# A diffusion backbone on one core: scan products in a written order, like tile shapes together, no fill-in products

## Chip, core and metric

The kernel runs on one core of one Trainium2 chip. The metric is the device time of one execution in microseconds (us), shown as the median of three runs. Engines are named as in the profile: PE is TensorE's matmuls and PEld its weight loads, DVE is VectorE, ACT is ScalarE, POOL is GpSimd, SP is SyncE, which issues the DMAs.

## What is computed

Four layers over 256 latent and 256 context tokens of width 1024; layer i has the mixer i mod 3 (attention, RWKV-7 time mixing, pooling), each followed by a squared-ReLU MLP. The change lies in layer 1, RWKV-7, whose core is a recurrence over the tokens, run forwards and backwards for 16 heads of 64 channels:

```
def step(state, inp):
    r_t, w_t, k_t, v_t, kk_t, a_t = inp
    sa = jnp.einsum("bhvk,bhk->bhv", state, kk_t)
    state = (state * w_t[:, :, None, :]
             - sa[..., None] * (kk_t * a_t)[:, :, None, :]
             + v_t[..., None] * k_t[:, :, None, :])
    return state, jnp.einsum("bhvk,bhk->bhv", state, r_t)

for d in range(N_DIRS):
    rev = d == 1
    s_ctx, yc = _wkv_scan(zero, r_c, dec_c[d], key_c[d], v_c, kk_c, a_c[d], rev)
    _, yl = _wkv_scan(s_ctx, r_l, dec_l[d], key_l[d], v_l, kk_l, a_l[d], rev)
```

The two directions' outputs are summed, normalised per head (a group norm), given a bonus term and a gate, and multiplied by an output matrix.

## The kernel before, in words

`rwkv_scan` does the recurrence in chunks of 64 tokens. Work is cut into 16 units n: for each of 8 pairs of heads (`cc`), first the context half (s = 1), then the latent half (s = 0). A unit has both heads, both directions and 4 chunks (`q`); within a chunk the recurrence becomes products of 64x64 matrices and one triangular inverse. A unit passes through stages, and the loop over n works on five units at a time: in iteration n stand, in this order, `levels` of unit n+1, `chain` of n, `front_c` of n+2, `finish_a` of n, `chunks` of n+1, `front_b` of n+3, `front_a` of n+4 and the group norm of n (`STAGES`).

- `front_a` (L907) makes decays and keys: small products, Tanh and Exp on ACT, a running sum `cum` on DVE.
- `front_b` (L947) makes `KB` and `AR`, their products (`pre<-AR,KB`, L961) and the masked matrices `NG` (L966), which go to DRAM. `base` (L1008) reads their 16x16 diagonal blocks back, inverts them by small DVE operations (L1025 to L1034) and fetches the result as `X` and `XT`.
- `front_c` (L971) transposes `KB`, `AR` and the values (L982 to L996).
- `levels` (L1044) first makes a product of `VU` and `NG` (L1061), copied into `XR`; then it widens the inverse in two levels (L1057): `inv<-X,NG`, masked into `Tm`, then `inv<-XT,Tm` (and `inv<-Tm,XT`), by which DVE updates `XT` (L1082, once per level) and `X`.
- `chunks` (L1086) multiplies `XR` by `XT` (L1094) in two halves; ACT copies each to `G` and, scaled, to `VU` (L1097, L1099); `inv<-NG,G` (L1103) gives `P` and `Rp` on DVE (L1109, L1110); then `Q` (L1117, L1119) and the first part of the output sum `yps` (L1124).
- `chain` (L1129) carries the state `S` over the 4 chunks: a product on PE (L1142), an update on DVE (L1147), a product into `yps` (L1151).
- `finish_a` (L1155) centres the output and takes its variance; `inverse_std` and `finish_b` (L1168, L1173) finish the group norm after every second pair of heads (at n = 3, 7 and 11), and after each of the last two pairs; an ACT table load stands ahead of them.

A tile scheduler orders each engine's queue; the program's order of stages is only its preference, so products of different stages alternate in PE's queue. `warm` (L876) puts in 128x256 products whose result nobody reads (L880, the fill-in products): 2 after L1061, 3 after `inv<-X,NG`, 4 after `inv<-XT,Tm` and 3 after each product of the chain (`WARM`). The `inv` products share two PSUM banks, the `pre` products two, `lora` has one. After the scan `rwkv_output` multiplies the gated output by the output matrix (`pre<-kvr,KB` and `pre<-kvr,AR`, L248); the scheduler lets its first products run among the scan's last iterations.

Below, **P** is the start of DVE's first L1109 of a unit and **XT2** the end of DVE's second L1082.

Of the kernel before, what the change touches and what calls it, by code (L numbers as in the profile page):

```python
# [6 lines left out]
F32 = mybir.dt.float32  # L7
# [13 lines left out]
class Kern:  # L21
# [793 lines left out]
    def rwkv_scan(self, R, W, U, ps, psu, K, V, Rr, hid, xr):  # L815
# [19 lines left out]
        g = lambda dd: 1 - dd  # L835
# [46 lines left out]
        with self.pool("rwDram", 1, space=bass.MemoryType.DRAM) as dr:  # L882
# [24 lines left out]
            def front_a(cc, s, w2):  # L907
# [6 lines left out]
                nc.vector.scalar_tensor_tensor(kkn, kc[:, sl], v["k_k"][:, cc:cc + 1], pk[:, :T], op0=ALU.mult, op1=ALU.mult)  # L914
                tw = W.tile([128, 2, T], F32, name="tw")
# [29 lines left out]
                return dict(kkn=kkn, E=E, lam=lam, iL=iL, key=key, b=ta)  # L945

            def front_b(cc, s, st, it):  # L947
# [4 lines left out]
                NG = U.tile([128, 2, 2, 4, 3, 64], F32, name="NG", tag="NG", bufs=2)  # L952
                for dd in range(2):
# [4 lines left out]
                    nc.gpsimd.tensor_mul(AR[:, :, 1, g(dd)], tv(Rr[cc][:, s * T:s * T + T]), E[:, dd, :, 1:65])  # L958
                for dd in range(2):
# [8 lines left out]
                    nc.sync.dma_start(full(Ls[it % NB], g(dd)), NG[rows(g(dd)), dd, :, :, 0].rearrange("p h q x -> p (h q) x"))  # L968
                st.update(AR=AR, KB=KB, NG=NG)

            def front_c(cc, s, st):  # L971
# [7 lines left out]
                for dd in range(2):  # L979
# [4 lines left out]
                    nc.scalar.copy(NG[:, dd, :, :, 2], pn.rearrange("p q (h x) -> p h q x", h=2))  # L984
                pn = pt().rearrange("p (q x) -> p q x", q=4)
# [3 lines left out]
                nc.scalar.copy(XR[:, :, :, 0], pn.rearrange("p q (h x) -> p h q x", h=2))  # L989
                vr = W.tile([128, T], F32, name="vr", tag="t1")  # L990
# [6 lines left out]
                for dd in range(2):  # L997
                    for par in range(2):
                        nc.scalar.copy(VU[rows(dd), dd, par::2].rearrange("p q h x -> p q (h x)"), pv[rows(par), dd])
                ks = W.tile([128, T], F32, name="ks")  # L1000
# [5 lines left out]
                st.update(XR=XR, VU=VU)  # L1006
# [36 lines left out]

            def levels(st):  # L1044

                NG, VU, XT, X, XR = [st[n] for n in ("NG", "VU", "XT", "X", "XR")]
# [3 lines left out]
                def bank():  # L1050
                    return psu.tile([128, 2, 4, 64], F32, name="inv", tag="inv", bufs=2)
# [7 lines left out]
                p = bank()  # L1059
                for dd, hh, q in units:  # L1060
                    nc.tensor.matmul(p[rows(g(dd)), hh, q], lhsT=NG[rows(dd), dd, hh, q, 0], rhs=VU[rows(dd), dd, q, hh],  # L1061
                                     start=True, stop=True)
                warm("k")
                nc.scalar.copy(XR[:, :, :, 1], p)
                for lv, m in enumerate((16, 32)):
# [10 lines left out]
                    else:  # L1076
                        nc.scalar.mul(cols(Tz, 0), cols(p, 0), odd[:, 0:1])
                    p = prod(of(Tz), of(XT))
# [4 lines left out]
                    if lv == 0:  # L1083
                        nc.vector.tensor_sub(cols(X, 0), cols(X, 0), cols(p2, 0))

            def chunks(st):  # L1086
# [3 lines left out]
                for hh in range(2):  # L1090
# [7 lines left out]
                    for dd in range(2):  # L1098
                        nc.scalar.mul(VU[rows(g(dd)), dd, :, hh], p[rows(g(dd)), :, 1], -1.0)  # L1099
                P = U.tile([128, 2, 4, 64], F32, name="P", tag="P", bufs=2)  # L1100
# [10 lines left out]
                p = psu.tile([128, 2, 4, 64], F32, name="inv", tag="inv", bufs=2)  # L1111
                Q = U.tile([128, 2, 4, 64], F32, name="Q", tag="Q", bufs=2)
                yp = psu.tile([128, 2, T], F32, name="yps", tag="yps", bufs=1)
                for dd in range(2):
                    for q in range(4):
                        for hh in range(2):
                            nc.tensor.matmul(p[rows(hh), dd, q], lhsT=NG[:, dd, hh, q, 2], rhs=VU[:, dd, q, hh],  # L1117
                                             start=True, stop=True)
                nc.vector.tensor_mul(Q, p, st["lam"].unsqueeze(3).broadcast_to([128, 2, 4, 64]))  # L1119
                start = [True, True]  # L1120
                for dd in range(2):
                    for q in range(4):
                        for hh in range(2):
                            nc.tensor.matmul(yp[rows(hh), dd, q * 64:q * 64 + 64], lhsT=VU[:, dd, q, hh],  # L1124
                                             rhs=NG[:, dd, hh, q, 1], start=start[hh], stop=True, skip_group_check=True)
                            start[hh] = False
                st.update(P=P, Rp=Rp, Q=Q, yp=yp)

            def chain(st, s, S):  # L1129
                P, Rp, Q, yp, lam = [st[n] for n in ("P", "Rp", "Q", "yp", "lam")]  # L1130
                for q in range(4):
                    if s == 1 and q == 0:
                        S = U.tile([128, 2, 64], F32, name="S", tag="S", bufs=3)
                        nc.gpsimd.tensor_copy(S, Q[:, :, 0])
                        continue
                    So = S
                    if not (s == 0 and q == 3):
# [8 lines left out]
                        for dd in range(2):  # L1146
                            nc.vector.scalar_tensor_tensor(S[:, dd], p[:, dd], lam[:, dd, q:q + 1], Q[:, dd, q],  # L1147
                                                           op0=ALU.mult, op1=ALU.add)
                    for dd in range(2):
# [3 lines left out]
                return S  # L1153

            def finish_a(cc, s, yp, y2):  # L1155
# [4 lines left out]
                nc.vector.tensor_add(y, y, yp[:, 1, ::-1])  # L1160
                yp = pt(0).rearrange("p (a t) -> p a t", a=2)
                nc.tensor.matmul(yp[:, 0], lhsT=c["center"], rhs=y, start=True, stop=True)
                nc.scalar.square(y, yp[:, 0])
                nc.scalar.copy(y2[0][:, sl], yp[:, 0])
                nc.tensor.matmul(yp[:, 1], lhsT=c["meanH"], rhs=y, start=True, stop=True)
                return nc.scalar.copy(y2[1][:, sl], yp[:, 1])
# [6 lines left out]
            def finish_b(cc, w2, y2, r):  # L1173
# [7 lines left out]
                nc.gpsimd.tensor_add(y, y, V[cc])  # L1181
                pf = pt(0)
# [242 lines left out]
```

## Time and profile before

| | |
|---|---|
| median of 3 runs | 2548.38 us (2546.79 to 2548.97) |
| the profiled execution | 2542.58 us |
| its span in the profile | 2540.7 us |
| PE busy / DVE / ACT / POOL, share of the span | 95% / 68% / 43% / 13% |
| fill-in products: first start, last start | 849.0 us, 1358.2 us |

The span is the time in which the engines work; the execution is 1.9 us longer. The table's busy shares are averages over layers with different limits: PE's 95% comes mostly from the long dense products of the MLPs. The scan takes about a fifth of the span.

### The profile page before, as it was taken

What the parts mean: (1) busy time and instruction counts of PE and PEld (TensorE: products, weight loads), DVE (VectorE), ACT (ScalarE), POOL (GpSimd) and SP (SyncE); (2) the same over time, 40 slices, a digit from 0 to 9 for tenths busy, and PEclk for the clock granted to TensorE, in tenths of its full rate; (3) what the DMA queues carried; (4) which work ended last, traced back from release to release, by engine and by line L of the source; (5) the groups of instructions that cost most, each with busy time, mean ns of one, the idle gap of its engine ahead of it and who ended that gap; (6) DMA issues with size and microseconds to landing.
All of it is one profiled execution on the core that took longest, in us unless ns stands there. A gap on an engine that the chain in (4) does not pass through costs nothing.

```text
span 2540.7 us, 42517 instructions
## 1 busy us (share of the span) xinstructions
PE 2418.3 (95%) x17392; PEld 1941.5 (76%) x17392; DVE 1723.3 (68%) x2813; ACT 1101.3 (43%) x2015; POOL 341.5 (13%) x406
## 2 busy tenths in 40 slices
PE   7999999999799999999999899999899999898999
PEld 5556888888577777777777788888788888766999
DVE  5777787674786666666664777664787683787555
ACT  4677523323564334343443523323533323476443
POOL 0110101100202222222210101100011001010110
PEclk9999999999899999999999999999899999999999
DMA  7530355553123311211132255452155553203453
GB/s 276 187 112 32 131 198 187 188 185 116 60 83 96 73 37 38 38 32 37 32 69 99 84 199 198 166 183 85 68 196 182 184 197 116 72 26 108 166 181 135
DMA packets 154834, 308.36 MB, mean 121 GB/s; under 512 B 107152, under 2 KB 111632, under 8 KB 122768
## 3 DMA queue, kind: packets, MB, share of 16 engines
q1 hardware_dynamic: 154640, 305.65, 35.7%
q8 instruction: 137, 2.24, 0.4%
q14 instruction: 57, 0.47, 0.1%
HBM read 294.58 MB, written 11.03 MB: 120 GB/s over the span
## 4 chain that ended last, share of the span: by engine, by line
PE 80%; DVE 11%; ACT 6%; issue 2%; POOL 1%; DMA 1%; SPq 0%; DVEq 0%; ACTq 0%; POOLq 0%
PE mm L248 51%; PE mm L259 3%; PE warm L880 2%; PE inv L1057 2%; PE po L618 2%; PE pre L248 2%; PE pre L961 2%; DVE wL L238 1%; PE pt L613 1%; PE sc L602 1%; PE rps L870 1%; PE inv L1103 1%; ACT wH L237 1%; PE yps L1124 1%; DVE cum L930 1%
## 5 line engine op out<-in xcount | busy, mean ns | idle before, releaser
L238 DVE TENSOR_TENSOR wL<-wraw,wH 128x1024 fp32r<-128x1024 f32 (+1 forms) x364 | 415.1, 1144 | 270.6 <-ACT wH L237 269.7
L237 ACT CAST wH<-wraw 128x1024 fp32r<-128x1024 f32 (+1 forms) x364 | 341.8, 943 | 448.0 <-PE mm L248 425.8
L248 PE MATMUL mm<-hH,wH 128*128 128x512 f32 (+1 forms) x1296 | 471.0, 364 | 2.3 <-ACT wH L237 2.1
L248 PE MATMUL mm<-hH,wL 128*128 128x512 f32 (+1 forms) x1296 | 470.7, 363 | 2.5 <-DVE wL L238 2.4
L248 PE MATMUL mm<-hL,wH 128*128 128x512 f32 (+1 forms) x1296 | 465.6, 360 | 0.0
L248 PE MATMUL mm<-uH,wH 128*128 128x512 f32 (+1 forms) x1072 | 380.6, 355 | 0.0
L248 PE MATMUL mm<-uL,wH 128*128 128x512 f32 (+1 forms) x1072 | 379.4, 355 | 0.3
L248 PE MATMUL mm<-uH,wL 128*128 128x512 f32 (+1 forms) x1072 | 379.5, 354 | 0.0
L188 DVE SCALAR_TENSOR_TENSOR acc<-wraw,sc_sb,acc 128x2048 f32<-128x2048 f32 x126 | 302.2, 2414 | 51.6 <-DMA wraw<-in_w_mod 46.3
L379 POOL TENSOR_TENSOR usq<-relu 128x512 f32<-128x512 f32 (+1 forms) x128 | 144.5, 1130 | 1252.6 <-ACT relu L377 1252.6
L248 PEld LDWEIGHTS mm<-hH,wH 128*128 128x128 f32 x1296 | 244.8, 189 | 56.0 <-ACT wH L237 11.7
L248 PEld LDWEIGHTS mm<-hH,wL 128*128 128x128 f32 x1296 | 244.9, 189 | 42.8 <-DVE wL L238 5.1
L248 PEld LDWEIGHTS mm<-hL,wH 128*128 128x128 f32 x1296 | 244.7, 189 | 35.8 <-issue 0.2
L248 PEld LDWEIGHTS mm<-uL,wH 128*128 128x128 f32 x1072 | 202.3, 189 | 29.1 <-DVE uL L383 1.1
L248 PEld LDWEIGHTS mm<-uH,wH 128*128 128x128 f32 x1072 | 202.7, 189 | 28.4
L248 PEld LDWEIGHTS mm<-uH,wL 128*128 128x128 f32 x1072 | 202.7, 189 | 28.3
L326 DVE SCALAR_TENSOR_TENSOR x<-mm,mod,x 128x256 f32<-128x256 f32 x272 | 121.9, 479 | 132.3 <-PE mm L248 132.1
L377 ACT ACTIVATE relu<-mm 128x512 f32<-128x512 f32 (+1 forms) x128 | 69.2, 544 | 296.4 <-PE mm L248 283.3
L259 PE MATMUL mm<-hH,wH 128*128 128x256 f32 (+1 forms) x232 | 75.5, 328 | 26.4 <-ACT hH L309 15.4
L382 ACT CAST uH<-usq 128x512 fp32r<-128x512 f32 (+1 forms) x128 | 72.7, 569 | 46.1 <-POOL usq L379 46.1
L383 DVE TENSOR_TENSOR uL<-usq,uH 128x512 fp32r<-128x512 f32 (+1 forms) x128 | 80.4, 629 | 0.8
L880 PE MATMUL warm<-busy 128*128 128x256 f32 x400 | 77.3, 318 | 0.0
(342 smaller groups left out, 3906.9 us busy)
## 6 DMA issues: line engine op xcount, KB each, us to landing
wraw<-in_w_mod SPq DMA_DIRECT2D x96, 1024.0 KB, 4.9
wraw<-in_w_in SPq DMA_DIRECT2D x64, 1024.0 KB, 5.8
wraw<-in_w_out SPq DMA_DIRECT2D x64, 1024.0 KB, 5.8
wraw<-in_w_qk SPq DMA_DIRECT2D x10, 1024.0 KB, 4.8
wraw<-in_w_rkv SPq DMA_DIRECT2D x9, 1024.0 KB, 4.8
wraw<-in_w_ao SPq DMA_DIRECT2D x16, 512.0 KB, 4.0
Ls<-NG SPq DMA_DIRECT2D x32, 128.0 KB, 2.6
XT<-Xs SPq DMA_DIRECT2D x32, 128.0 KB, 3.2
```

The source lines that it names most:

```text
L188: nc.vector.scalar_tensor_tensor(acc, raw, self.sc[:, k, s:s + 1], acc, op0=ALU.mult, op1=ALU.add)
L237: nc.scalar.copy(h[:, sl], raw[:, sl])
L238: nc.vector.tensor_sub(l[:, sl], raw[:, sl], h[:, sl].bitcast(F32))
L248: self.nc.tensor.matmul(ps, lhsT=a[:, k], rhs=b, start=(n == 0), stop=(n == 3 * nk - 1))
L259: self.nc.tensor.matmul(ps[:, lo:hi], lhsT=a[:, k], rhs=b, start=(k == z == 0), stop=(k == nk - 1 and z == 2))
L326: self.nc.vector.scalar_tensor_tensor(self.x[o][:, a:b], ps, G[:, o, s:s + 1], self.x[o][:, a:b], op0=ALU.mult, op1=ALU.add)
L377: nc.scalar.activation(r[:, :n], ps[:, :n], AF.Relu)
L379: nc.gpsimd.tensor_mul(u2[:, :n], r[:, :n], r[:, :n])
L382: nc.scalar.copy(uH[:, :n], u2[:, :n])
L383: nc.vector.tensor_sub(uL[:, :n], u2[:, :n], uH[:, :n].bitcast(F32))
L618: nc.tensor.matmul(po[hf * 64:hf * 64 + 64], lhsT=vn[:, k0 + kc, (2 * P + hf) * 64:(2 * P + hf) * 64 + 64], rhs=pts[hf][:, kc].rearrange(" ...
L880: self.tc.keep_in_program_order(nc.tensor.matmul(wb[:, 0:T], lhsT=busy[:, 0:128], rhs=busy, start=True, stop=True))
```

## The change

The stages become generators that stop after each step (`yield`), and a list `STEPS` names, step by step, the order in which an iteration takes them; `k` is now the first product of `levels`, cut out as a step of its own (`mv`), and `G` the gate product of the group norm, taken in the next iteration. From iteration 0 on, `ordered` ties each PE instruction to the one before, so PE's queue follows the list; the other engines' queues are still ordered by the scheduler. `WARM` is empty: none of the 400 fill-in products is left. Everything computed stays the same.

```diff
+    def ordered(self, on, steps):
+        traced = self.nc.cur_bb.bb.instructions
+        n = len(traced)
+        steps()
+        for i in list(traced[n:]) if on else ():
+            if i.engine == mybir.EngineType.PE:
+                if self.pe:
+                    self.tc.add_manual_dep(i, self.pe.name, mybir.DependencyInfo(mybir.DependencyClass.NoSync,
+                                           mybir.DependencyReason.DATA), reason="ordered")
+                self.pe = i
...
+            def mv(st):
+                NG, VU, XR = [st[n] for n in ("NG", "VU", "XR")]
+                p = bank()
+                for dd, hh, q in units:
+                    nc.tensor.matmul(p[rows(g(dd)), hh, q], lhsT=NG[rows(dd), dd, hh, q, 0], rhs=VU[rows(dd), dd, q, hh],
+                                     start=True, stop=True)
+                warm("k")
+                nc.scalar.copy(XR[:, :, :, 1], p)
+                yield
...
-STAGES = (("l", 1), ("x", 0), ("c", 2), ("f", 0), ("h", 1), ("b", 3), ("a", 4), ("g", 0))
-
-WARM = [dict(k=2, l=3, m=4, x=3)]
+AHEAD = dict(l=1, k=1, x=0, c=2, f=0, h=1, b=3, a=4, g=0, G=-1)
+STEPS = [[(z, AHEAD[z]) for z in order.split()] for order in (
+    "k l l l l c c c c c h h h h h b b b b a a",
+    "l G x l x x b l k l G G x x x h x h x f c c f c c c h f b h h a b b a g")]
+ORDERED = 0
+WARM = [{}]
```

Three places in the engines' queues. First PE's, from the second level of `levels` to the first product of `chunks`, in an iteration whose `chain` is of an s = 0 unit. Before:

```order
L1057 MATMUL inv<-X,NG 64x64 x16
L880 MATMUL warm<-busy 128x256 x3
L1142 MATMUL chain<-S,P 64x64 x3
L1057 MATMUL inv<-XT,Tm_6370 64x64 x16
L880 MATMUL warm<-busy 128x256 x10
L1142 MATMUL chain<-S,P 64x64
L880 MATMUL warm<-busy 128x256 x3
L1151 MATMUL yps<-Rp,S 64x64 x6
L982 MATMUL pre<-c_base,KB 128x128 x5
L1151 MATMUL yps<-Rp,S 64x64 x2
L982 MATMUL pre<-c_base,KB 128x128
L1094 MATMUL inv<-XR,XT 64x128 x2
```

The same place now (L1087 is the levels' product, L1071 the `mv` step, L1174 the chain, L1120 the `XR`, `XT` product):

```order
L1087 MATMUL inv<-X,NG 64x64 x16
L1071 MATMUL inv<-VU,NG 64x64 x16
L1087 MATMUL inv<-XT,Tm_6370 64x64 x16
L1184 MATMUL yps<-Rp,S 64x64 x4
L1174 MATMUL chain<-S,P 64x64 x4
L1184 MATMUL yps<-Rp,S 64x64 x4
L1120 MATMUL inv<-XR,XT 64x128 x16
L1184 MATMUL yps<-Rp,S 64x64 x4
L998 MATMUL pre<-c_base,KB 128x128 x8
```

The 16 fills are gone, the `VU`, `NG` product has come here from between the `front_b` and `front_a` products, and the `XR`, `XT` product stands ahead of the `KB` transposes. In an iteration whose chain is of an s = 1 unit, one chain product stands between the two halves of L1120.

Second, PE's queue from there to the product that P waits for. Before:

```order
L1094 MATMUL inv<-XR,XT 64x128 x2
L987 MATMUL pre<-c_base,AR 128x128 x4
L1094 MATMUL inv<-XR,XT 64x128 x2
L996 MATMUL pre<-c_base,kvr 128x128 x2
L996 MATMUL pre<-c_base,vr 128x128 x2
L1004 MATMUL pre<-ks,c_base 128x256
L1162 MATMUL pre<-sqr,c_rwkvB 128x256
L1094 MATMUL inv<-XR,XT 64x128 x8
L1165 MATMUL pre<-sqr,c_base 128x256
L1094 MATMUL inv<-XR,XT 64x128 x4
L1103 MATMUL inv<-NG,G_9580 64x128
```

Now:

```order
L1120 MATMUL inv<-XR,XT 64x128 x16
L1184 MATMUL yps<-Rp,S 64x64 x4
L998 MATMUL pre<-c_base,KB 128x128 x8
L1197 MATMUL pre<-sqr,c_rwkvB 128x256
L1004 MATMUL pre<-c_base,AR 128x128 x4
L1014 MATMUL pre<-c_base,kvr 128x128 x2
L1014 MATMUL pre<-c_base,vr 128x128 x2
L1024 MATMUL pre<-ks,c_base 128x256
L1130 MATMUL inv<-NG,G_10143 64x128 x16
```

The `XR`, `XT` product stands in one piece and all products on whole 128x128 tiles follow it in one run; the second product of `finish_a` (L1165, now L1201) has moved behind the `NG`, `G` product. On ACT, the copies to `G` and `VU` now stand ahead of those of `finish_a` and `front_c`; before they stood behind.

Third, DVE's queue at P in the period after a group norm (`ssum` and `sqr` hold what ACT's Ln and Exp give). Before:

```order
L1176 SCALAR_TENSOR_TENSOR yvar_7491<-yvar_7491,ssum_6777 128x512
L1109 TENSOR_TENSOR P_8754<-c_rwkvB_6359,inv_8756 128x256
L1110 TENSOR_TENSOR Rp_8755<-AR_7996,inv_8756 128x256
L1109 TENSOR_TENSOR P_8754<-c_rwkvB_6359,inv_8757 128x256
L1110 TENSOR_TENSOR Rp_8755<-AR_7996,inv_8757 128x256
L914 SCALAR_TENSOR_TENSOR kkn_8887<-kvr_5482,vecs_sb_64,pre_8885 128x256
L1177 SCALAR_TENSOR_TENSOR yvar_7491<-yvar_7491,ssum_6777 128x512
L1119 TENSOR_TENSOR Q_8779<-inv_8778,lam_7681 128x512
```

Now:

```order
L1136 TENSOR_TENSOR P_8646<-c_rwkvB_6359,inv_8648 128x256
L1137 TENSOR_TENSOR Rp_8647<-AR_7724,inv_8648 128x256
L1136 TENSOR_TENSOR P_8646<-c_rwkvB_6359,inv_8649 128x256
L1137 TENSOR_TENSOR Rp_8647<-AR_7724,inv_8649 128x256
L1212 SCALAR_TENSOR_TENSOR yvar_7448<-yvar_7448,ssum_6777 128x512
L1212 SCALAR_TENSOR_TENSOR yvar_8216<-yvar_8216,sqr_6778 128x512
L980 TENSOR_TENSOR NG_8672<-pre_8673,c_rwkvB_6359 128x4x128
```

The group norm's operations have moved behind P, two of them ahead of the `NG` masks. In that period DVE's second XT update also stands behind two more of `base`'s large operations than in the others.

## Rows read from the trace of the kernel before

**Rows 1.** The page, parts 1 and 2: engines' busy times, clock in 40 slices.
```profile
PE 2418.3 (95%) x17392; PEld 1941.5 (76%) x17392; DVE 1723.3 (68%) x2813; ACT 1101.3 (43%) x2015; POOL 341.5 (13%) x406
...
PEclk9999999999899999999999999999899999999999
```

**Rows 2.** Busy time in stretches from P to XT2 or XT2 to P.
```profile
core 0: us, PE busy (x) PEld busy (x) DVE busy (x) ACT busy (x) POOL busy (x), PEclk, DMA share, GB/s
1034.65:1054.92 20.27, 18.44 (x345) 15.36 (x346) 16.34 (x42) 4.38 (x9) 6.52 (x9) 1.00 0.15 29
1054.92:1066.10 11.18, 10.82 (x124) 7.91 (x125) 4.30 (x10) 6.56 (x17) 1.16 (x3) 1.00 0.32 59
1066.10:1087.09 20.99, 19.16 (x339) 15.94 (x340) 16.42 (x42) 4.38 (x9) 6.81 (x10) 0.92 0.13 28
1087.09:1098.24 11.15, 10.63 (x123) 8.08 (x123) 4.20 (x9) 6.44 (x17) 1.17 (x3) 1.00 0.28 51
...
1119.31:1133.03 13.72, 12.80 (x159) 9.82 (x158) 4.92 (x12) 10.11 (x22) 1.16 (x3) 1.00 0.27 49
1133.03:1155.90 22.87, 21.57 (x320) 15.56 (x319) 21.38 (x50) 8.47 (x14) 10.16 (x12) 1.00 0.17 37
...
1166.68:1188.61 21.93, 20.10 (x338) 16.83 (x339) 16.42 (x42) 4.38 (x9) 6.52 (x9) 0.86 0.14 26
1188.61:1200.93 12.32, 11.96 (x131) 9.05 (x131) 4.30 (x9) 6.56 (x17) 1.16 (x3) 0.97 0.30 55
...
1298.79:1362.07 63.28, 63.03 (x996) 49.34 (x996) 29.61 (x79) 17.93 (x42) 1.96 (x2) 1.00 0.20 43
869.15:1298.79 429.64, 400.71 (x6015) 314.95 (x6017) 289.58 (x687) 165.16 (x370) 112.61 (x171) 0.97 0.21 40
```

**Rows 3.** The chain that ended last, one period: start, us, what.
```profile
1052.03 0.55 PE warm L880 x3
...
1053.88 1.38 PE warm L880 x10
...
1055.52 0.55 PE warm L880 x3
...
1064.54 1.53 PE inv L1103 x29
```

**Rows 4.** Timeline of PE in that period.
```profile
1046.41 1.10 PE L1057 MATMUL inv<-Tm,XT 64*64 64x64 f32 x32
...
1050.88 1.15 PE L1057 MATMUL inv<-X,NG 64*64 64x64 f32 x32 [1.83 <-DVE Zb L1027]
...
1057.72 0.44 PE L1094 MATMUL inv<-XR,XT 64*64 64x128 f32 x4
...
1060.49 1.09 PE L1094 MATMUL inv<-XR,XT 64*64 64x128 f32 x16
```

**Rows 5.** Timeline of DVE in that period.
```profile
1053.54 1.04 DVE L1030 TENSOR_TENSOR tb<-Nb,Zb 64x512 f32<-64x512 f32 x1
1054.52 0.40 DVE L1082 TENSOR_TENSOR XT<-XT,inv 128x256 f32<-128x256 f32 x1
...
1056.78 0.27 DVE L1147 SCALAR_TENSOR_TENSOR S<-chain,lam,Q 128x64 f32<-128x64 f32 x1
...
1066.10 0.42 DVE L1109 TENSOR_TENSOR P<-c_rwkvB,inv 128x256 f32<-128x256 f32 x1 [4.64 <-PE inv L1103]
```

**Rows 6.** Timeline of ACT: two rows of that period, two of a group norm.
```profile
1061.77 0.39 ACT L1097 COPY G<-inv 128x256 f32<-128x256 f32 x1
1062.17 0.77 ACT L1099 ACTIVATE VU<-inv 64x256 f32<-64x256 f32 x2
...
1128.18 1.28 ACT L93 ACT_TABLE_LOAD   x1
...
1130.54 0.71 ACT L1170 ACTIVATE ssum<-yvar,gneps 128x512 f32<-128x512 f32 x1
```

**Rows 7.** The fill-in products alone, busy time in the last 63 us of the scan.
```profile
1298.79:1362.07 63.28, 11.24 (x59) 7.96 (x59) 1.00 0.20 43
```

More of the change, by code (lines that the diff above doesn't have):

```diff
@@ L1058, in prod @@
                     return p
[L1059 to L1064, printed above, removed]
                 for lv, m in enumerate((16, 32)):
@@ L1110, in chunks @@
                     nc.vector.tensor_sub(Rp[:, dd], AR[:, :, 1, g(dd)], p[:, :, 0])
-                p = psu.tile([128, 2, 4, 64], F32, name="inv", tag="inv", bufs=2)
-                Q = U.tile([128, 2, 4, 64], F32, name="Q", tag="Q", bufs=2)
+                yield
                 yp = psu.tile([128, 2, T], F32, name="yps", tag="yps", bufs=1)
[L1114 to L1119, printed above, removed]
                 start = [True, True]
@@ L1126, in chunks, with chain @@
                             start[hh] = False
+                yield
+                p = psu.tile([128, 2, 4, 64], F32, name="inv", tag="inv", bufs=2)
+                Q = U.tile([128, 2, 4, 64], F32, name="Q", tag="Q", bufs=2)
+                for dd in range(2):
+                    for q in range(4):
+                        for hh in range(2):
+                            nc.tensor.matmul(p[rows(hh), dd, q], lhsT=NG[:, dd, hh, q, 2], rhs=VU[:, dd, q, hh],
+                                             start=True, stop=True)
+                nc.vector.tensor_mul(Q, p, st["lam"].unsqueeze(3).broadcast_to([128, 2, 4, 64]))
                 st.update(P=P, Rp=Rp, Q=Q, yp=yp)
-            def chain(st, s, S):
+            def chain(st, s):
+                nonlocal S
                 P, Rp, Q, yp, lam = [st[n] for n in ("P", "Rp", "Q", "yp", "lam")]
@@ L1213, in stage @@
                         clear()
-                    front_b(cc, s, st, n)
-                    base(st, n)
+                    return front_b(cc, s, st, n)
                 if op == "c":
-                    front_c(cc, s, st)
+                    return front_c(cc, s, st)
+                if op == "k":
+                    return mv(st)
                 if op == "l":
-                    levels(st)
+                    return levels(st)
                 if op == "h":
@@ L1229, in stage, with norms @@
                         ycs.append([W.tile([128, NT], F32, name=n, tag=n, bufs=2) for n in ("yc", "yvar")])
-                    last[0] = finish_a(cc, s, st["yp"], ycs[cc])
-                if op == "g" and s == 0 and (cc % 2 or cc >= SINGLE):
+                    return finish_a(cc, s, st["yp"], ycs[cc])
+                return norms(cc, s)
+            def norms(cc, s):
+                two = []
+                if s == 0 and (cc % 2 or cc >= SINGLE):
                     two = list(zip((cc - 1, cc) if cc < SINGLE else (cc,), (self.ssum, self.sqr)))
@@ L1236, in stage @@
                     for c2, r in two:
-                        finish_b(c2, w2s[c2][1], ycs[c2], r)
+                        finish_b(c2, ycs[c2], r)
+                for c2, r in two:
+                    yield
+                    gate(c2, w2s[c2][1], ycs[c2][0])
+                yield
+            self.pe = None
+            live = {}
             for n in range(-4, len(order)):
@@ L1242, in rwkv_scan @@
                     self.unpark()
-                for op, ahead in STAGES:
-                    stage(op, n + ahead)
+                live = {"G": live["g"]} if "g" in live else {}
+                for op, ahead in STEPS[n >= 0]:
+                    if not 0 <= n + ahead < len(order):
+                        continue
+                    if op == "w":
+                        warm(ahead)
+                        continue
+                    if op == "G":
+                        if op in live:
+                            self.ordered(n >= ORDERED, lambda: next(live[op], None))
+                        continue
+                    if op not in live:
+                        live[op] = stage(op, n + ahead)
+                    self.ordered(n >= ORDERED, lambda: next(live[op], None))
+                traced = len(nc.cur_bb.bb.instructions)
+                assert all(next(z, live) is live for y, z in live.items() if y != "g") and traced == len(nc.cur_bb.bb.instructions)
+            for _ in live["g"]:
+                pass
             return out
```

51 lines of the change are left out of this document (32 added, 19 removed).

## The prediction

> **What bounds the kernel now.** I read the page first: PE is busy for 95% of the span and its clock is nearly full throughout [rows 1]. That share comes mostly from the MLPs; what the change is worth must be read from the scan, so next I cut the scan at two events of each unit, P (P and Rp begin) and XT2 (the inverse is done), and read the busy time between them [rows 2]. From unit 0's P to unit 13's there are 13 periods in 429.64 us. A plain one has 20.27 us from P to XT2 and 11.18 us from XT2 to the next P. In the first stretch DVE is busy for 16.3 of 20.3 us and sets the end: its large L1030 ends at 1054.58 and the XT update starts at 1054.52, in queue order and not after PE [rows 5]. In the second DVE works 4.3 of 11.2 us and waits 4.64 us for the NG, G product [rows 2, 5].
>
> Third, the chain of waits of that period: three groups of fill-in products lie on it, 0.55, 1.38 and 0.55 us [rows 3]. The first stands beside the ACT copy of Tm, so not all of it can be won. Of the others the reader is to see what comes behind: XT2 is at 1054.92, the first XR, XT product starts at 1057.72 [rows 4], 2.80 us late, behind fills, chain and transposes. ACT then copies G at 1061.77 only [rows 6], behind the copies of front_c.
>
> **Part 1, XT2 to P.** Now only yps, chain and yps stand ahead of the XR, XT product, 24 records; at the pace of the fully packed 64x64 groups (32 records in 1.15 us, rows 4) 0.8 us, most of it before XT2: it starts 0.25 us after XT2. Each half takes 1.09 us with its tail [rows 4]. So ACT's first G copy starts at 1.5, and G (0.39) and VU (0.77) twice [rows 6] end at 3.8. Meanwhile PE waits for the last state update: DVE's S at 1056.78 is 1.86 us after XT2 [rows 5], so yps goes at 2.35 us, the KB transposes end at 3.9, finish_a's copy (behind VU) and sum at 4.65, its product goes at 4.8, transposes and ks follow to 7.3 (the ks product waits for ACT's XR copy, which frees its PSUM bank), and NG, G takes 1.7 (1.53 in rows 3 for 29 records of 32). P comes at 9.2 against 11.18: -2.0 us. With an s = 1 chain a chain product stands between the two halves and waits for the same S: the second half goes at 2.7 instead of 1.15, and P comes at 10.5 against 11.15 [rows 2]: -0.6 us. After a group norm the stretch was 13.72 us [rows 2], because a 1.28 us table load [rows 6] and the norm's copy stood ahead of ACT's second G; these now come behind: about 9.7, -4.0. The 13 periods have 3 of the first kind, 7 of the second, 3 of the third: -6.0 - 4.2 - 12.0 = -22.2 us. Bounds: 0, if each wait is only renamed; 2.8 us for each period, -36, if the whole delay of the first XR, XT goes.
>
> **Part 2, P to XT2.** The VU, NG product (16, 1.15 us) leaves the first part, where PE works without a gap, and hides the Tm copy instead of three fills. But PE now has the NG masks' PSUM banks to wait for, so tw comes at about 8.1 us after P against 8.5. The levels' first mask moves ahead of cum. From there to XT2 DVE's queue holds the same operations, and DVE is the bound: -0.35 us in 10 plain periods, -3.5 us (from 0 to -1.2 each, the product's own time).
>
> In the three periods after a group norm DVE now meets two norm operations ahead of the NG masks. They need ACT's table load (1.28), two Ln and one Exp (0.61 to 0.71 each, starts in rows 6), begun about 1 us after P, so DVE stands still from 1.4 to about 4.3 us after P, and what hangs on the masks (front_a's products, through the PSUM banks) comes as late. XT2 is also two operations of base later, partly covered. I take +3.0 us on 22.87 [rows 2], +9.0; bounds 0 (the norm's 5 us of DVE work was there before) and +4.5 each.
>
> **Part 3, the tail.** From unit 13's P to the scan's end PE is busy 63.03 of 63.28 us [rows 2], filled by the output product. There a fill costs what it takes: 59 of them [rows 7], at 0.11 to 0.14 us from start to start (10 in 1.38, rows 3), 6.5 to 8 us. Some waits of the chain will stay open: -5 us, bounds 0 and -8.
>
> The fills outside of these terms cost nothing: DVE hides them. Base's DMAs keep their places behind the NG masks; SP's queue is not the bound in any stretch read here. The ramp before unit 0's P has only 15 or 16 fills and the same DVE work; I take 0 (bounds -2, +2).
>
> **Part 4, the clock.** Between the levels' first products (done at 1047.5) and the next one at 1050.88, PE had 4 fills, a chain step and then idled 1.83 us [rows 4]. With that same gap the granted clock stayed at 1.00, the 2.4 GHz level, in one period, and in the next its mean fell to 0.92, part of it at 1.2 GHz [rows 2]. A fall costs 20.99 - 20.27 = 0.7 us; the long one at 0.86 costs (21.93 - 20.27) + (12.32 - 11.18) = 2.8 us. The mean of 0.97 over the 13 periods means that 6%, about 26 us, was at the low level; the long fall holds 6.9 of them and paid 2.8, the other 19 at the price of the 0.92 row (0.72 us lost for 3.4 at the low level) 4: about 7 us are paid already. Now the fills and the transposes leave the gap, and the products before it end a little earlier: PE idles about 3 us. I expect a fall in every plain period, a third of them long, and 0.2 more for each since the VU, NG product has entered the stretch behind the gap: 10 x (0.67 x 0.7 + 0.33 x 2.8 + 0.2) = 16 us, less the 7 paid: +9 us. Bounds: -7 (no fall any more) and +29 (13 long ones, 36, less 7).
>
> The Trainium skill speaks against the change here: "TensorE: Matmul & The Clock Gate", section "HAM oscillation — how this bites in real kernels", has a loop whose waits send the clock back to half in every pass, and its advice is to leave no such gaps. By that rule the fourth part stands at its upper end; the trace shows falls at this place, but not in each pass.
>
> **The sum.** -22.2 - 3.5 + 9.0 - 5 + 9 = -12.7 us, against the profiled execution's 2542.6 (span 2540.7 and 1.9 around it): 2529.9. That execution was 5.8 us below the runs' median, so on the median of 2548.4 I forecast 2535.7, rounded 2536.
>
> **Rivals.** (1) The clock holds: the order leaves PE dense enough that falls become no more frequent. For it: the same gap of 1.83 us passed at full clock in one of two periods [rows 2, 4]. Then part 4 is between -7 and 0: 2520 to 2527, say 2525. (2) The order stalls: a fixed queue makes PE stand before each late input (finish_a's sum, the PSUM bank of ks, S in the middle of the XR, XT product), where the scheduler put something else in; what is won ahead of XT2's reader is given back before NG, G. For it: the chain of waits ran through ACT copies for 2 us there already, and I find PE waiting at three places. Against it: G is ready much earlier. Part 1 then keeps only the 4.0 us of the group norms: -12 - 3.5 + 9 - 5 + 9 = -2.5, about 2546. (3) The clock decides, on the other side: every gap brings a long fall, at 2.8 us in each of 13 periods, from the levels' products on into the next stretch: -21.7 + 36 - 7 = +7, rounded 2556. It makes the change slower from an average price of about (21.7 + 7) / 13 = 2.2 us a period on. For it: the fills' only purpose there can be the clock, and the gap grows by half; against it: the products behind the gap are dense and after the fall at 0.92 the clock was back at 1.00 in the next stretch [rows 2].
>
> **Chances.** Forecast 0.38, rival 1 0.22, rival 2 0.17, rival 3 0.23. A measurement here tells 0.2%, 5 us, from no change. The forecast's own range, 2526 to 2545, reaches into no change with about 0.05; rival 2 lies there with 0.10 and gives 0.05 to faster and 0.02 to slower; rival 3 is slower but for 0.03. Faster 0.22 + 0.33 + 0.05 = 0.60, same 0.18, slower 0.22. The range takes rival 1 and most of rival 3: 2518 to 2558.
>
> **What would show it.** XT2 to the first XR, XT product below 0.5 us; XT2 to P near 9.2 and 10.5 us in turn, and below 10 after a group norm; P to XT2 near 20 us at full clock, near 26 after a norm, with DVE waiting for ACT's Exp just behind P; a mean clock below 1.00 in every plain P to XT2, and of about 0.94 over the 13 periods. PE's records fall by the 400 fills, its busy share in the last 63 us stays full and that stretch is about 5 us shorter. I am wrong if XT2 to P stays at 11 us (rival 2), if the clock's mean is 0.97 or more (rival 1), or if plain P to XT2 is above 22 us with the clock at 0.86 or less (rival 3).

## The result, and the profile after

The changed kernel takes 2519.38 us (median of 4 runs, 2517.41 to 2521.33) against 2547.59 for the kernel before beside it: a ratio of 0.989, 95% interval [0.9876, 0.9904], 28 us faster. The forecast was 2536. The profiled execution took 2519.62 us, with a span of 2517.8; the profiled execution of before lay 5 us under its median, so between the two traces only 22.9 of the 28 us can be followed.

From unit 0's P to unit 13's the trace has 413.5 us for 429.6 [rows 2], -16.1; behind that it is 7.4 us shorter, and unit 0's P comes 0.6 later. The 13 stretches from XT2 to P went from 152.2 us in all to 119.2; those from P to XT2 went from 277.4 to 294.3, and all of that is in the three periods after a group norm (69.6 to 86.5). The other ten are called plain.

The page of after, parts 1 and 2 (it answers rows 1):

```profile
PE 2333.9 (93%) x16992; PEld 1888.4 (75%) x16992; DVE 1724.5 (68%) x2813; ACT 1100.9 (44%) x2015; POOL 342.6 (14%) x406
...
PEclk9999999999899998899999999999999999999999
```

PE lost 84 us of busy time, far more than the span did. Where it now stands idle the stretches show; they answer rows 2 (unit 6 from P to XT2 and on to P; unit 8, the same; an odd unit's XT2 to P; the period after a norm; the whole scan part):

```profile
core 0: us, PE busy (x) PEld busy (x) DVE busy (x) ACT busy (x) POOL busy (x), PEclk, DMA share, GB/s
1028.47:1048.91 20.44, 16.45 (x348) 14.12 (x348) 16.10 (x42) 4.97 (x10) 6.39 (x9) 0.92 0.10 18
1048.91:1057.31 8.40, 7.06 (x93) 5.95 (x93) 4.27 (x9) 5.86 (x16) 1.10 (x3) 1.00 0.31 53
...
1088.79:1109.21 20.42, 15.14 (x348) 12.81 (x348) 16.09 (x42) 4.97 (x10) 6.40 (x9) 1.00 0.10 19
...
1146.61:1156.21 9.60, 7.64 (x113) 6.28 (x107) 4.36 (x12) 6.49 (x17) 1.17 (x3) 1.00 0.45 85
...
989.56:1018.87 29.31, 25.33 (x326) 17.93 (x328) 24.95 (x52) 11.82 (x19) 10.61 (x12) 0.71 0.15 32
869.75:1283.27 413.52, 325.88 (x5649) 267.40 (x5647) 292.82 (x686) 164.46 (x369) 112.20 (x170) 0.91 0.21 41
```

Read the first and third row together: unit 6 has a fall of the clock in it (0.92), unit 8 none (1.00), and both take 20.4 us. PE works in them for 16.5 and 15.1 us, so it has room for the slower stretch. The last row against that of before: PE idle 28.9 us then (429.64 - 400.71), 87.6 now (413.52 - 325.88).

The chain of waits of unit 6's period from XT2 on (start, us, what; it answers rows 3):

```profile
1047.55 1.03 DVE tb L1049
1048.58 0.34 DVE XT L1107
...
1049.06 1.10 PE inv L1120 x16
...
1052.38 0.27 ACT sqr L1193
1052.66 0.43 DVE sqr L1194
...
1053.14 0.71 PE pre L1197 x2
...
1054.52 0.50 ACT XR L1006
...
1055.06 0.70 PE pre L1024 x2
1055.76 1.52 PE inv L1130 x32
```

Up to XT2 it runs through DVE, with base's large L1049 ahead of the XT update, as before. Behind XT2 it goes through finish_a's copy, sum and product, ACT's copy to XR and the ks product, none of which the NG, G product (L1130) uses: it only stands behind them in PE's queue. PE, DVE and ACT there (timelines; they answer rows 4 to 6), and DVE and ACT just behind P in the period after a norm:

```profile
1043.63 1.42 PE L1087 MATMUL inv<-X,NG 64*64 64x64 f32 x26 [1.73 <-DVE X L1109]
...
1049.06 1.96 PE L1120 MATMUL inv<-XR,XT 64*64 64x128 f32 x32 [0.56 <-DVE XT L1107]
...
1053.14 0.70 PE L1197 MATMUL pre<-sqr,c_rwkvB 128*128 128x256 f32 x2 [0.84 <-DVE sqr L1194]
```

```profile
1048.51 0.40 DVE L1107 TENSOR_TENSOR XT<-XT,inv 128x256 f32<-128x256 f32 x1
...
1057.31 0.42 DVE L1136 TENSOR_TENSOR P<-c_rwkvB,inv 128x256 f32<-128x256 f32 x1 [0.22 <-PE inv L1130]
...
993.77 0.69 DVE L1212 SCALAR_TENSOR_TENSOR yvar<-yvar,ssum 128x512 f32<-128x512 f32 x1 [2.79 <-ACT ssum L1207]
```

```profile
1050.18 0.37 ACT L1123 COPY G<-inv 128x256 f32<-128x256 f32 x1 [2.83 <-PE inv L1120]
...
990.59 1.28 ACT L105 ACT_TABLE_LOAD   x1
...
993.13 0.61 ACT L1207 ACTIVATE ssum<-ssum 128x512 f32<-128x512 f32 x1
```

The first XR, XT product starts 0.15 us behind XT2 (2.80 before), ACT's first G copy at 1.27 (6.85 before). The 2.79 us of DVE behind the norm's P are the wait that was foreseen.

### The profile page after: what moved, and what is told of

It is laid out like the page before. It is cut to its first block, busy times and chain, and to the rows that moved or that the text cites. A ratio compares the mean times of both kernels' runs of the same rounds, so it can differ in the third digit from the quotient of the medians.

```text
span 2517.8 us, 41717 instructions
## 1 busy us (share of the span) xinstructions
PE 2333.9 (93%) x16992; PEld 1888.4 (75%) x16992; DVE 1724.5 (68%) x2813; ACT 1100.9 (44%) x2015; POOL 342.6 (14%) x406
## 4 chain that ended last, share of the span: by engine, by line
PE 75%; DVE 14%; ACT 6%; issue 2%; DMA 1%; POOL 1%; SPq 0%; DVEq 0%; ACTq 0%; POOLq 0%
PE mm L260 52%; PE mm L271 3%; PE po L630 2%; PE pre L260 2%; DVE wL L250 1%; PE pt L625 1%; PE sc L614 1%; PE pre L975 1%; PE rps L882 1%; DVE NG L980 1%; ACT wH L249 1%; PE inv L1130 1%; DVE tb L1044 1%; DVE Zb L1046 1%; PE pre L931 1%
## 5 line engine op out<-in xcount | busy, mean ns | idle before, releaser
L260 PE MATMUL mm<-uL,wH 128*128 128x512 f32 (+1 forms) x1072 | 379.4, 355 | 0.3
L1087 PE MATMUL inv<-X,NG 64*64 64x64 f32 x1024 | 46.2, 253 | 34.9 <-DVE X L1109 34.4
```

Source lines behind the costliest of these rows:

```text
L260: self.nc.tensor.matmul(ps, lhsT=a[:, k], rhs=b, start=(n == 0), stop=(n == 3 * nk - 1))
L1087: nc.tensor.matmul(p[u[0], hh, q], lhsT=lhs(*u), rhs=rhs(*u), start=True, stop=True)
```

## The experiments

All of them in one table: time, ratio to runs of before beside it, and of each trace the time from unit 0's P to unit 13's, PE's busy time in it, the mean of P to XT2 in the ten plain periods, and the mean of XT2 to P in all 13 (us).

| kernel | time | ratio | scan | PE busy | P to XT2 | XT2 to P |
|---|---|---|---|---|---|---|
| before | 2547.6 | | 429.6 | 400.7 | 20.8 | 11.7 |
| after | 2519.4 | 0.989 | 413.5 | 325.9 | 20.8 | 9.2 |
| no_fills | 2476.2 | 0.972 | 373.8 | 334.5 | 20.0 | 7.6 |
| order_fills | 2555.2 | 1.003 | 440.9 | 389.5 | 22.5 | 9.8 |
| few_fills | 2524.7 | 0.990 | 412.2 | 383.9 | 21.4 | 9.4 |
| half_fills | 2612.1 | 1.024 | 496.3 | 459.6 | 20.0 | 17.1 |
| c_first | 2547.2 | 1.000 | 427.6 | 399.2 | 23.3 | 7.6 |
| c_first_B | 2535.8 | 0.995 | 416.4 | 393.2 | 22.3 | 7.9 |
| free_order | 2483.1 | 0.975 | 376.6 | 321.1 | 21.2 | 6.1 |
| c_early | 2523.2 | 0.990 | 417.9 | 333.4 | 21.8 | 8.7 |
| c_early_B | 2507.0 | 0.984 | 405.4 | 331.1 | 20.1 | 9.2 |
| c_early_mB | 2503.3 | 0.983 | 399.2 | 324.7 | 19.9 | 9.8 |
| gap_fills | 2548.9 | 1.000 | 438.9 | 353.5 | 22.6 | 9.8 |
| gap_few | 2518.0 | 0.988 | 413.4 | 334.1 | 20.8 | 9.1 |
| no_exp | 2534.7 | 0.995 | 406.2 | 323.5 | 20.6 | 9.5 |
| no_fills_m | 2486.5 | 0.976 | 384.3 | 343.1 | 20.1 | 7.1 |
| free_B | 2479.6 | 0.973 | 370.8 | 326.9 | 20.2 | 6.6 |
| free_fB | 2475.6 | 0.972 | 369.8 | 322.4 | 19.7 | 7.2 |
| no_fills_B | 2477.9 | 0.972 | 373.8 | 333.9 | 20.1 | 7.6 |
| no_fills_hB | 2482.4 | 0.974 | 379.4 | 338.4 | 21.2 | 5.6 |

**The two halves of the change apart.** In the kernel before, no_fills has `WARM = [{}]`; in the kernel after, order_fills has `WARM = [dict(k=2, l=3, m=4, x=3)]`.

> The kernel before with its 400 fill-in products left out, the scheduler's own order kept. My theory now is that most of the gain comes from the written order (the XR, XT product directly behind XT2 and ACT's G and VU copies ahead of the others), and that the fills alone are worth about 5 to 7 us in the last 63 us of the scan, where PE is busy without a gap, and a few us ahead of the XR, XT product: 2538 us, with XT2 to P still near 10.5 us. Rival: the fills were what stood between XT2 and the XR, XT product, and without them the scheduler's order does as well as the written one: 2520 us, XT2 to P at 8.4 to 9.6. Second rival, the clock: without fills in the gap between the levels' products every fall costs 0.7 to 2.8 us: 2550 or more.

> The changed kernel with the old fills put back at their places (2 behind the VU, NG product, 3 and 4 behind each level's products, 3 behind each chain product), the written order kept. Theory: P to XT2 stays at 20.4 us, because DVE sets it, and has fewer clock falls; XT2 to P grows by the fills that stand between the last level product and the XR, XT product and between its halves, 0.4 to 0.8 us in each of 13 periods (5 to 10 us), and the tail by some 6 us: about 2532. Rival: the fills keep the clock up and so pay for themselves: 2520 or less.

Leaving out the fills alone makes the old kernel 71 us faster (ratio 0.9721 [0.9706, 0.9735]); the written order gives 43 of them back, and with the fills it is slower than before (1.0032 [1.0021, 1.0043]). The first rival held, and more than held; my theory of the order fell. Order_fills missed both of its sides: P to XT2 did not stay at 20.4 us but rose to 22.5, with the XT update behind two or three large operations of base in the plain periods. The fills and the order do not add up, but each keeps its sign: leaving out the fills wins 71 us in the scheduler's order and 36 in the written one (2555.2 to 2519.4), and the written order loses 43 us without fills and 8 with them. No_fills has XT2 to P at 7.33 us in unit 6. The scheduler put 14 to 16 of a unit's 16 transpose records ahead of XT2 in the plain periods, where before it put 1 or 2; with half of the fills (few_fills, below) it is 6 to 12. Its stretches (unit 6, a norm period, the scan) and PE in unit 6:

```profile
1010.96:1030.33 19.37, 16.58 (x354) 13.97 (x355) 15.47 (x42) 5.62 (x12) 6.95 (x11) 1.00 0.23 46
1030.33:1037.66 7.33, 7.17 (x91) 5.06 (x91) 4.76 (x10) 5.14 (x15) 0.72 (x1) 1.00 0.18 20
977.99:1003.28 25.29, 22.72 (x325) 16.35 (x324) 22.70 (x50) 9.88 (x17) 10.30 (x12) 0.87 0.23 50
869.27:1243.03 373.76, 334.51 (x5666) 262.01 (x5666) 288.34 (x686) 164.92 (x370) 112.98 (x168) 0.96 0.23 45
```

```profile
1020.11 0.87 PE L982 MATMUL pre<-c_base,KB 128*128 128x128 f32 x6
...
1024.38 0.38 PE L987 MATMUL pre<-c_base,AR 128*128 128x128 f32 x2
...
1030.72 0.65 PE L1094 MATMUL inv<-XR,XT 64*64 64x128 f32 x8
```

PE's busy time in the scan falls by 66.2 us and the scan by 55.9, of which 54.0 lie in XT2 to P. PE was busy for 93% of the scan before, and 62.6 us of that (325 records) were fills: this points to PE as the bound, and c_first_B below shows it where fills and transposes both stand ahead of XT2.

**What a fill costs.** Few_fills has `WARM = [dict(k=1, l=2, m=2, x=1)]`, half_fills fills of 128 columns; c_first writes stage c ahead of l in `STAGES`; c_first_B also cuts base in two:

```diff
-STAGES = (("l", 1), ("x", 0), ("c", 2), ...
+STAGES = (("c", 2), ("l", 1), ("B", 2), ("x", 0), ...
...
+                with self.tc.issue_after(xt2[0].ins) if xt2[0] else ExitStack():
+                    nc.vector.tensor_mul(tm, by_row(N16[:, 0:8, 8:16]), by_col(Z[:, 8:16, 8:16]))
```

> The kernel before with half of its fills (1 behind the VU, NG product, 2 behind each level's products, 1 behind each chain product, 200 in all). Theory: a fill costs the PE time that it takes, wherever it stands: half of the 71 us come back, 2505 to 2518. Rival: only the fills between XT2 and the XR, XT product cost (those come in groups of 10 and 3, now 5 and 1), the rest is hidden: then XT2 to P falls but P to XT2 does not, and the time is 2525 or more; or, if the clock needs many of them, 2545 and more clock falls.

> The kernel before with every fill kept at its place but half as wide (128 columns for 256). Theory: PE's own time is what bounds the scan (93% busy between unit 0's P and unit 13's, 62.6 us of it fills; without them 55.9 us less), so a fill costs the PE time that it takes: about half of the 71 us come back, 2505 to 2515, with the clock as before. Rival: a fill costs by being an instruction in the queue that is ordered in between (its count and place), whatever its width: 2535 or more.

> The kernel before with all its 400 fills, with one edit: the stage front_c is written first in each iteration, so the scheduler prefers its transposes to the fills when both are ready. The kernel without fills was 71 us faster, with XT2 to P at 7.1 to 9.0 us, and there the KB, AR and V transposes stand in PE's waits ahead of XT2. Theory: the fills cost mainly because they take those waits and push 18 transposes and ks (2.4 us and ACT's copies behind them) past XT2; then with the transposes first XT2 to P falls to about 8.5 us although every fill stays, and the time to about 2515. Rival: the fills cost what they last on the chain (0.55 + 1.38 + 0.55 us in a period); then the time stays within 10 us of before, 2537 to 2547.

> c_first (all 400 fills, transposes preferred to them, 2547 us, P to XT2 23.3 us, XT2 to P 7.0) with base cut in two and its large operations tied behind DVE's last XT update. Theory: two effects are mixed in c_first; the fills' PE time lies beside DVE's work, and what made P to XT2 long was DVE's order (three large operations of base ahead of the update, 2.8 us): P to XT2 falls to about 20.5 us, 2510 to 2520. Rival: the fills' PE time is itself on the path to XT2, since transposes and fills together fill PE's waits: P to XT2 stays above 22 us, 2535 or more.

Half of the fills give back 23 of the 71 us, between the theory's range and the rival's time, and with the rival's pattern: XT2 to P fell, P to XT2 did not. Its clock fell oftener, 11 times for 7, so it does not price a fill exactly. Half_fills came out far on its rival's side but did not test its theory: a narrow fill takes nearly as long. Three of them took 0.55 us, three wide ones 0.62, both at the full clock (half_fills, then before):

```profile
1089.83 0.55 PE L880 MATMUL warm<-busy 128*128 128x128 f32 x3
```

```profile
1051.96 0.62 PE L880 MATMUL warm<-busy 128*128 128x256 f32 x3
```

The scheduler also made another order: no transpose stands ahead of XT2, the first XR, XT product comes 5.2 to 10.7 us behind XT2, and the clock's mean is 0.83. So whether a fill costs by the PE time that it takes or by its place in the queue, half_fills does not tell.

C_first is the telling one. XT2 to P fell to 7.0 us as expected, but P to XT2 rose by as much and the time did not move, the rival's side. Both stretches of an odd unit, and DVE ahead of XT2:

```profile
1069.25:1092.56 23.31, 21.99 (x374) 18.05 (x374) 19.42 (x46) 7.29 (x16) 7.47 (x11) 1.00 0.16 31
1092.56:1099.57 7.01, 6.96 (x101) 5.27 (x102) 1.69 (x5) 3.43 (x10) 0.44 (x2) 1.00 0.41 71
```

```profile
1089.28 1.04 DVE L1030 TENSOR_TENSOR tb<-Nb,Zb 64x512 f32<-64x512 f32 x1
1090.35 0.68 DVE L1031 TENSOR_REDUCE tc<-tb 64x64 f32<-64x512 f32 x1
1091.07 1.16 DVE L1032 TENSOR_TENSOR tb<-Zb,tc 64x512 f32<-64x512 f32 x1
1092.16 0.40 DVE L1082 TENSOR_TENSOR XT<-XT,inv 128x256 f32<-128x256 f32 x1
```

Two things are in it: PE is full, and the XT update stands behind three large operations of base for one before [rows 5]. C_first_B takes the second away: P to XT2 is still 22.2 to 22.3 us in every plain period, the rival's side, 2535.8. There DVE stands ready and waits for PE, 1.4 to 1.9 us in every plain period:

```profile
1085.64 0.42 DVE L1088 TENSOR_TENSOR XT<-XT,inv 128x256 f32<-128x256 f32 x1 [1.90 <-PE inv L1063]
```

So DVE's time ahead of XT2 hides the fills or the transposes, not both.

**What the tie costs.** Free_order is the changed kernel with `ORDERED = 99`: the same steps, PE's queue left to the scheduler. C_early keeps the tie and moves front_c's steps in the list; c_early_B ties base's large operations behind XT2 as above; c_early_mB also ties the norm's first DVE operation behind the second pair of NG masks and moves both gate products to the end of the levels. The list of c_early:

```diff
-    "l G x l x x b l k l G G x x x h x h x f c c f c c c h f b h h a b b a g")]
+    "l G x l c x x c b l k c l G G x x x c h x h x f c f h f b h h a b b a g")]
```

> The changed kernel, its steps traced in the written order and without fills, but without the tie that holds PE's queue to that order: the scheduler may again take what is ready. What is seen so far: the kernel before without fills takes 2476 us with PE idle for 39 us between unit 0's P and unit 13's; the written order takes 2519 with PE idle for 88 us there. Theory: it is the tie that costs 43 us, by waits in PE's queue; without it PE idles 40 us there again: 2475 to 2490. Rival: the loss lies in the order of the steps as traced (k cut out of the levels, the gate products an iteration later), which also sets priorities for the scheduler: 2505 or more.

> The changed kernel with only the place of front_c's steps in the list altered: the two KB transposes into the waits behind the first level's products, the AR and V transposes behind the second level's, ks behind the first XR, XT half. Theory: the written order loses 43 us to the scheduler's order without fills because it keeps all transposes behind XT2; P to XT2 is set by DVE (20.4 us) and hides them: XT2 to P falls from 8.4 and 9.6 us to 6 to 6.5, P to XT2 grows by about 0.7 because one more operation of base stands ahead of the XT update: 2.0 us for each of 13 periods and some in the tail, 2485 to 2495. Rival: XT2 to P is set by ACT's G and VU copies and the chain, not by PE's transposes: it stays above 8 us and the time above 2510.

> c_early, and base cut in two: its large operations (1.03 + 0.67 + 1.07 + 0.67 + 0.38 us) are tied behind DVE's last XT update, as the scheduler put them without fills. Theory: P to XT2 falls to about 19.4 us, as without fills, and the large operations lie in XT2 to P, where DVE worked 4.3 us of 8.4 and now has room for 3.8 less: -1.0 to -1.7 us a period against c_early, 2470 to 2480. Rival: DVE then comes late to finish_a's sum and to S, which PE waits for in its fixed order, and XT2 to P grows by as much: the same as c_early.

> c_early_B, and the group norm's DVE operations tied behind the second pair of NG masks after P, with both gate products at the end of the levels. Theory: the 2.79 us for which DVE stood for ACT's Exp ahead of the masks vanish, and the gates no longer stand ahead of the level's products: P to XT2 after a norm falls by about 4 us three times, 2460 to 2470. Rival: the norm's 6 us of DVE work are the whole of it and the wait is only moved to tw: no change against c_early_B, within 4 us.

Free_order came out as its theory said: 2483.1 (0.9745 [0.9728, 0.9761]), -36.9 us in the scan, of which XT2 to P is -39.9. PE in its unit 6:

```profile
1036.63 1.96 PE L1120 MATMUL inv<-XR,XT 64*64 64x128 f32 x32 [1.82 <-DVE XT L1107]
1038.52 0.70 PE L1197 MATMUL pre<-sqr,c_rwkvB 128*128 128x256 f32 x2
...
1039.80 1.79 PE L1130 MATMUL inv<-NG,G 64*64 64x128 f32 x32
```

The NG, G product starts 3.2 us behind the XR, XT product; with the tie it is 6.6 (1049.06 to 1055.69). Three hand-made orders did not find this: c_early shortened XT2 to P in even units to 7.3, but P to XT2 grew by as much (the update now behind two operations of base, falls of the clock moved behind XT2) and it was no faster than after. C_early_B got its 19.4 us from P to XT2 in six of the ten plain periods, and 16 us on c_early as its theory had, though not its time; XT2 to P stayed long, above all behind a norm (11.6 to 12.9 us). C_early_mB shortened P to XT2 after a norm by 4.0 us and lost 3.1 of them behind XT2, where the XR, XT product came up to 8.9 us late, behind the gate products; 2503.3 is its rival's side.

**The clock.** Gap_fills and gap_few put 16 and 6 fills into the changed kernel at one place, ahead of the second level, where PE waits 1.73 us.

```diff
-    "l G x l x x b l k l ...
+    "l G x l x x w b l k l ...
+WARM = [{}] * 4 + [dict(w=16)]
```

> The changed kernel with 16 fill-in products in one place alone, ahead of the second level's first product, where PE waits 1.73 us for DVE's X update in every iteration. Theory: a fall of the clock behind that gap costs nothing, since DVE sets XT2 (units 6 and 8 of the changed kernel both have 20.42 to 20.43 us from P to XT2, one with a fall and one without); so the falls go, from about 20 in the scan to a few, and the time stays within 0.2%, 2515 to 2521. Rival, the prediction's own price: 0.7 us for a short fall and 2.8 for a long one, some 1.0 us for each of 13 periods and more behind a norm: 2500 to 2508.

> gap_fills with 6 fills in place of 16: they fit in PE's wait of 1.73 us, and DVE's order stays that of the changed kernel. Theory: falls of the clock cost nothing here, as P to XT2 is set by DVE; P to XT2 stays at 20.4 us and the time within 0.2% of 2519 whether the falls go or stay. Rival, the prediction's price of a fall: with the falls gone 8 to 13 us are won, 2506 to 2511; or the fills' place alone costs, 2530.

Gap_fills missed: the scheduler put the XT update behind three operations of base (at 1060.17, with L1049 at 1057.43), P to XT2 rose to 22.26 us and the falls came behind XT2. Gap_few kept DVE's order: 11 falls for 16 in the 13 periods, and 2517.95 us for 2519.38, no change. Not all falls went, so it does not price those that stayed, the ones behind a norm among them. Its units 6 (with a fall) and 8 (without):

```profile
1027.84:1048.27 20.43, 17.35 (x354) 14.88 (x354) 16.10 (x42) 4.96 (x10) 6.40 (x9) 0.92 0.11 18
1088.09:1108.51 20.42, 16.13 (x354) 13.67 (x354) 16.08 (x42) 4.96 (x10) 6.40 (x9) 1.00 0.13 24
```

**The group norm.** In no_exp ACT multiplies by 0 for Ln and Exp; no_fills_m is no_fills with the norm's tie of c_early_mB.

> The changed kernel without the Ln and Exp of the group norm and the table loads that they bring: ACT writes zeros there with one multiplication by 0 for each, so the norm's output is not computed; DVE's and PE's work of the norm stays. Theory: after a norm, DVE stands 2.79 us just behind P for ACT's Exp, and this is a third of what the norm periods lost (P to XT2 of 28 to 29 us against 20.4): they fall to about 26 us, -2.3 us three times in the scan and some in the tail: 2508 to 2513. Rival: the loss comes from the long fall of the clock behind the gap and from the gate products in it; then P to XT2 stays above 28 and the time at 2519.

> The kernel before without fills, and the group norm's DVE operations tied behind the second pair of NG masks after P. There DVE waited 3.58 us for ACT's Exp just ahead of P (XT2 to P 9.0 us against 7.3 in units 4, 8 and 12). Theory: -1.7 us in each of three periods and nothing lost behind P: 2469 to 2473. Rival: P to XT2 after a norm grows by as much, since the norm's 6 us of DVE work only come later: 2475 to 2480.

In no_exp P to XT2 after a norm fell from 28.8 to 25.7 us, and the scan by 7.3, as expected. Its whole time did not: behind unit 13's P it is 25.7 us longer. Without the load ahead of the norm the Ln and Exp of a later stage each bring their own table, 42 loads for 12, 30 x 1.283 = 38.5 us of ACT; that these make the 25.7 us is likely, and not shown.

```profile
L277 ACT ACT_TABLE_LOAD x19 | 24.4, 1283 | 0.3
L278 ACT ACT_TABLE_LOAD x19 | 24.4, 1283 | 0.3
```

No_fills_m was 10 us slower than no_fills, worse than its rival: P to XT2 after a norm 30.6 us for 25.3.

**Versions that might be faster.** Free_B and no_fills_B add the cut of base; free_fB also moves `f` (`f c c f f c c c h b h h`); no_fills_hB also writes stage h ahead of c.

> The changed kernel without the tie on PE's queue (2483 us), and base's large operations tied behind DVE's last XT update. Without the tie P to XT2 was 20.8 to 21.1 us in plain periods with two large operations ahead of the update, and 19.4 in the kernel before without fills, where they stand behind. Theory: P to XT2 falls to about 19.4 and XT2 to P stays near 5.1 and 6.0, since DVE had room there: -1.5 us in 10 to 13 periods, 2463 to 2470. Rival: DVE has no room left there (it would work 7 of 5 to 6 us), so that P waits for DVE: no gain, 2480 to 2486.

> free_B, and finish_a's last step (the variance's product and copy) traced ahead of front_c's last steps and the NG, G product, so that ACT's Ln and Exp can begin about 1.5 us earlier. Theory: after a norm DVE waits for Exp by that much less: -1.5 us in each of three periods and in the two norms of the tail, so -4 to -7 against free_B. Rival: ACT takes the variance's copy only after the VU copies, as before, and the product delays P by 0.5 us in every period: +3 to +6.

> The kernel before without fills (2476 us), with base cut in two and its large operations tied behind the last XT update. Theory: in units of s = 0 (P to XT2 20.8 us against 19.4) the update stood behind one of them: -1.4 us in four or five periods, and as much after a norm: 2464 to 2470. Rival: the large operations then delay finish_a's sum and P: 2476 or more.

> no_fills_B, with the stage chunks written ahead of front_c and finish_a, so that the scheduler prefers the XR, XT and NG, G products to the transposes that stand between them. Theory: XT2 to P falls from 7.1 to 9.0 us to about 5.1 to 6, as in the changed kernel without its tie: -1.5 to -2 us a period on no_fills_B, 2440 to 2455. Rival: what is pushed back (transposes, ks, finish_a) lengthens P to XT2 by as much: 2464 to 2476.

Free_B won 3.5 us of the 13 to 20 hoped for: P to XT2 fell by 1.0, XT2 to P rose by 0.5. Free_fB won 4 more, as expected, and no_fills_B nothing, its rival's side. No_fills_hB has the shortest XT2 to P, 5.6 us, and pays for it in P to XT2, above all after a norm (31.6 us): 2482.4 is worse than its rival. The fastest are free_fB and no_fills, 2475.6 and 2476.2, not told apart; the second is the kernel before with one line changed.

## Why the prediction was right and wrong

The side was right, the size not (-28 for -12.7), and the reason was wrong. About 5 of the 15 us between are none of the terms: the forecast took the runs of after to lie 5.8 us above their profiled execution, as those of before did, and they do not (2519.38 and 2519.62). Between the two profiled spans it is -22.9 for -12.7, term by term:

- XT2 to P: -33.0 us for -22.2. The three kinds of period came to 8.4, 9.6 and 8.4 us where 9.2, 10.5 and 9.7 were worked out. That the product starts at XT2, ACT copies G at once and the norm's copies come behind was right; the steps behind it were each taken a little too long (finish_a's product starts 4.2 us behind XT2 for 4.8).
- P to XT2 in plain periods and the clock together: 0.0 us in ten periods for -3.5 and +9. The -3.5 did not come: at the full clock a plain period takes 20.42 us for 20.27. The falls came nearly as foreseen (in nine of the ten plain periods, 16 for 7 in all, mean 0.91 for the 0.94 foreseen), but their price was wrong: I took 0.7 to 2.8 us for each from two periods of before [rows 2]. There PE was busy for 19.2 of 21.0 us and DVE's XT update waited for it; now PE has room, and where DVE sets XT2 it ends in time at the 1.2 GHz level all the same. The Trainium skill's page "TensorE: Matmul & The Clock Gate", section "HAM oscillation — how this bites in real kernels", advises against such gaps. The falls that it describes are in this trace; of the eight plain P to XT2 with a fall six show no cost of it, two do (22.55 and 21.90 us), and one fall behind XT2 does (9.73 us for 8.40).
- P to XT2 after a norm: +16.9 us for +9.0. DVE's wait for Exp is there (2.79 us), and no_exp gives back 3.2 of the 5.6 us a period. The rest I did not price: two gate products stand ahead of the level's, 2.07 us each where the clock was 0.71 on average. What the gates and what the clock cost there, no run takes out alone.
- The last stretch: -7.4 us for -5; the ramp +0.6 for 0.

The step that failed is "The fills outside of these terms cost nothing: DVE hides them". I read DVE as the bound from P to XT2 and took PE's waits there as free room. That holds only while the clock is full: in seven of the 13 periods of before the XT update waits 0.4 to 1.6 us for PE, as in the one that I had for the price of a fall:

```profile
1086.67 0.42 DVE L1082 TENSOR_TENSOR XT<-XT,inv 128x256 f32<-128x256 f32 x1 [0.65 <-PE inv L1057]
```

Without the fills the scheduler fills that room with the transposes that stood behind XT2, and the whole term is -71 us. C_first and c_first_B show that fills and transposes compete for it. With the fills left in, the order does shorten XT2 to P, by 24.9 us (order_fills), but P to XT2 grows there by 36.2, the XT update behind more of base. In the whole time the gain that I gave to the order in the first part is therefore the fills'; what the order does without them is +43, by the waits of rival 2: finish_a's sum, ks and its PSUM bank ahead of the NG, G product. Free_order shows that the tie makes them, 36 of the 43 us. Rival 1's time, 2525, was the nearest, but its reason, a clock that holds, was not what happened: that the time came so near to it is chance.

Open stays why free_order and no_fills, with different orders, both end near 2480, and what a single fill costs, by its time or by its place.

## What to carry to other kernels

Work that is hidden is not free: ask what else could stand in its cover, and price a filler by taking it out alone. A queue tied to a written order makes every instruction wait for its forerunner's inputs; take the tie away before judging the order. And when a scheduler decides the other engines, a change on one moves them too: in these kernels, where DVE sets XT2, P to XT2 goes with the XT update's place among base's large operations, from 19.4 us (ahead of all, c_early_B) to 20.4 (behind one, after) and 22.3 (behind three, gap_fills).

## What was not expected of the hardware

A fill of 128 columns takes nearly as long as one of 256 (0.55 and 0.62 us for three). And a clock at half for a part of a stretch, 0.92 on average, left that stretch's time where it was (20.43 for 20.42 us in gap_few, PE busy for 17.4 and 16.1 of them), where before, with PE busy for 19.2 of 21.0 us, it added 0.7 us.
